# HGRN scores inside a hybrid encoder layer: levels 2 to 32 in blocks of 64 keys instead of 32

## The chip, the cores and the metric

The kernel runs on one core of a Trainium2 chip. A core has five engines that work beside each other and wait for each other by semaphores: PE (TensorE, matrix products; its weight loads are listed apart as PEld), DVE (VectorE), ACT (ScalarE), POOL (GpSimd) and SP (SyncE, which here issues DMAs). Products read SBUF and write PSUM, of which the kernel uses eight banks. The metric is the device time of one execution in microseconds (us), of which less is better.

## The reference, cut to what matters

One layer reads x (512 tokens, 2048 wide), projects it to all inputs of two mixers, RWKV-7 and HGRN2, joins their outputs and projects them back. HGRN2 has 8 heads of 128 key and 128 value dimensions. For each head the changed lines compute `att`, the scores of each token t against each earlier token s of the same stretch, with a decay per key dimension from s to t:

```python
b = jnp.cumsum(lf_c, axis=1)
diff = b[:, :, None] - b[:, None, :]
decay = jnp.where(causal, jnp.exp(jnp.where(causal, diff, 0.0)), 0.0)
att = jnp.einsum('btshd,bshd->btsh', q_c[:, :, None] * decay, k_c)
o_intra = jnp.einsum('btsh,bshv->bthv', att, i_c)
```

The decay differs by key dimension, so att is not one product of q and k. The kernel splits it by levels: at level w, a query in the second half of a stretch of 2w tokens meets a key in the first half, and the decay between them is the key's decay to the middle times the query's decay from the middle. With q and k scaled so, each level is a plain product. Level 1 joins neighbours, level 64 joins the two halves of 128 tokens; the diagonal (a token with itself) needs no decay.

## The kernel before

The projections are products of 128 by 128 weights with 512 columns, in fp32r, each made of three products of high and low parts (`three`, L431, and L1166 for the first ones). Between them lies the smaller work of the heads, in plain fp32. A program prints these functions below with their lines.

The order on every engine is fixed when the kernel is built, by a planner (class `Plan`). It keeps a clock for each engine, takes the next operation of each of several queues, and issues it when its inputs are ready by those clocks. An operation for PE goes between two projection products once its inputs are 0.35 us old; for products on part of the array (mode "narrow") it first waits a while so that several go together. `mm` gives a product's cost to the planner by its shape.

`hgrn_heads` works on two heads at once, so it runs four times (four pairs). For each head it holds q (`t` tile), f (the decays, later a copy of q or k), k, `near` (tag `nr`: the scores inside a small block, laid out as keys by queries), and later `dg` (a `t` tile with the scores of 4 stretches of 128 tokens).

- Level 1 and the diagonal: 16 products per head of 32 keys by 48 queries (32 undecayed and 16 decayed). Four lie side by side on the array, each writing 32 PSUM partitions (`blocks32`). The diagonal is cut out by a product with an identity of 32 columns, and level 1 is put in by `merge`.
- Then q and k are scaled from level to level (tensor_tensor, three per head and level). At every second level copies of q and k are kept (`kept`), so that two levels are multiplied in one PSUM bank (tag `mix`).
- Levels 2 and 4, then 8 and 16: per head and level 16 products of 32 keys by the 16 queries that lie in second halves, four side by side. Of the 32 x 16 scores only some belong to the level, and `merge` puts them in `near` by a copy under a mask (`cpred`, a table `hm` of one mask per level). After level 16 `near` is copied to the diagonal of `dg` in four parts of 32 partitions.
- Level 32: per head 8 products of 32 keys by 32 queries, which write partitions 0 to 31 and 64 to 95, so two lie side by side; two copies put them in `dg`. Level 64: per head 4 products of 64 by 64, two side by side, and two copies.
- `hgrn_out` multiplies `dg` with the values and adds the state of earlier stretches.

In the built program the projection products are `main` tiles, the heads' products `mix` (and `acc` in the RWKV scan). A whole-array product of the heads stands for RWKV state updates, transposes and the HGRN output.

Of the kernel before, what the change touches and what calls it, by code (L numbers as in the profile page):

```python
# [7 lines left out]
F32 = mybir.dt.float32  # L8
F32R = mybir.dt.float32r
U8 = mybir.dt.uint8  # L10
# [5 lines left out]
P = 128  # L16
T = 512
# [4 lines left out]
NHEAD = 8  # L22
C = 64
NCH = T // C
LEVELS = (1, 2, 4, 8, 16)
DECAY = math.exp(-0.5)
ALPHA = 2.0 ** 0.25
LN_EPS = 1e-5
# [206 lines left out]
def mixer_kernel(ctx, tc, head, x_r, w_all, par, up, ln_wb, consts, hmask, out):  # L235
# [72 lines left out]
    def mm(o, l, r, start=True, stop=True, **kw):  # L308
        m, n = size(l), size(r)
        narrow = m < P or l.shape[0] < P  # L310
        if r.dtype == F32R:
            cost = n / 2400 + 0.0135
        elif narrow:
            cost = 0.025 if m <= 32 else 0.06 if m <= 64 else 0.16
        else:
            cost = n / 600 + 0.005
        return Op([("pe", cost, lambda: pe.matmul(o, l, r, start=start, stop=stop, **kw))], [l, r], [o],  # L317
                  mode="narrow" if narrow else "main" if r.dtype == F32R else "whole")
# [20 lines left out]
    def tt(o, a, b, f=ALU.mult):  # L339
        return dve_op([a, b], o, lambda: dve.tensor_tensor(o, a, b, f),  # L340
                      base=0.16 if o.shape[0] < P and size(o) == C and o.tensor.name in tags else 0.07)
# [13 lines left out]
    def cpred(o, m, i):  # L355
        return dve_op([i], o, lambda: dve.copy_predicated(o, m, i))
# [142 lines left out]
        return u  # L499


    cst = cpool.tile([P, 3 * P + 32], F32, tag="cst", name="cst")
    ident = cst[:, 0:P]
    ones_blk = cst[:, P : 2 * P]
    mask_r = cst[:, 2 * P : 3 * P]
    eye32 = cst[:, 3 * P :]
    reset = cpool.tile([P, T], mybir.dt.bfloat16, tag="reset", name="reset")
    ones_r = cpool.tile([P, P], F32R, tag="ones_r", name="ones_r")
    hm = cpool.tile([P, 16 * len(LEVELS)], U8, tag="hm", name="hm")
    pr = cpool.tile([P, NPC], F32, tag="pr", name="pr")  # L510
    om = cpool.tile([P, 33], F32, tag="om", name="om")
    half = cpool.tile([P, 8, 8], F32, tag="half", name="half")
# [11 lines left out]
        return pr[:, base + p : base + p + 1]  # L524

    def constants():
        raw = st("ksq", [P, T])[:, : 16 * len(LEVELS)]
# [394 lines left out]
    def hgrn_heads(SS, h0):  # L922
# [4 lines left out]
        qqs, nrs = ([take(*a) for _ in SS] for a in (("q4", [P, 16, 48]), ("nr", [P, P])))  # L927
        totss = [[take("tot", [P, 256]) for _ in range(2)] for _ in SS]

        nears = [n.rearrange("p (c t) -> p c t", t=32) for n in nrs]  # L930
        for q, f, qq in zip(qs, fs, qqs):
            yield copy(qq[:, :, :32], q.rearrange("p (b t) -> p b t", t=32))
            yield tt(q, q, f)
            yield copy(qq[:, :, 32:], q.rearrange("p (b j two) -> p b j two", b=16, two=2)[:, :, :, 1])

        def blocks32(ps, n, k, moving):
            for b in range(16):
                c, g = b // 4, slice(b % 4 * 32, b % 4 * 32 + 32)
                yield mm(ps[g, c * n : c * n + n], k[:, b * 32 : b * 32 + 32], moving(b))

        def merge(near, m, w, scores):
            yield cpred(near.rearrange("p c (b two w) -> p c b two w", two=2, w=w)[:, :, :, 1],
                        hm[:, m * 16 : m * 16 + 16].rearrange("p (b w) -> p b w", w=w)[
                            :, None].to_broadcast([P, 4, 16 // w, w]),
                        scores.rearrange("p c (b w) -> p c b w", w=w))

        yield landed(*ks, *qqs)
        ps = take("mix")
        pss = [ps[:, 192 * i : 192 * i + 192] for i in range(2)]
        for pi, k, qq in zip(pss, ks, qqs):  # L950
            yield from blocks32(pi, 48, k, lambda b: qq[:, b])
        for pi, near in zip(pss, nears):
            scores = pi.rearrange("p (c t) -> p c t", t=48)
            yield tt(near, scores[:, :, :32], eye32[:, None, :].to_broadcast([P, 4, 32]))
            yield from merge(near, 0, 1, scores[:, :, 32:])
        drop(ps, *qqs)


# [1 line left out]
        for m, w in enumerate((2, 4, 8, 16, 32, 64, 128)):  # L960
# [13 lines left out]
            if w in (2, 8, 32):  # L974
# [2 lines left out]
                        halves = [a.rearrange("p (b two w) -> p b two w", two=2, w=w)[:, :, i] for a in (x, y)]  # L977
                        yield copy(*halves)
                continue
            if w == 16:  # L980
                yield room(t=2)
                dts = [take("t") for _ in SS]
                asking[0] -= 1
                dgs = [tiles(d) for d in dts]
                for d in dts:
                    yield memset(d, 0.0)
            yield landed(*qs, *ks, *kept)
            ps = take("mix")
            both = ((hw, kept, kept), (w, ks, qs))
            if w < 64:  # L990
                for v, (w1, k1, q1) in enumerate(both):
                    for i, (q, k) in enumerate(zip(q1, k1)):
                        yield from blocks32(ps[:, 64 * (2 * v + i) : 64 * (2 * v + i) + 64], 16, k,
                                            lambda b: q[:, b * 32 : b * 32 + 32].rearrange(
                                                "p (b two w) -> p b two w", two=2, w=w1)[:, :, 1])
                for v, (w1, k1, q1) in enumerate(both):
                    for i, near in enumerate(nears):
                        pi = ps[:, 64 * (2 * v + i) : 64 * (2 * v + i) + 64]
                        yield from merge(near, m + v, w1, pi.rearrange("p (c t) -> p c t", t=16))
# [4 lines left out]
            else:  # L1004

                for v, (w1, k1, q1) in enumerate(both):
                    n = P // (2 * w1)
                    for i, (q, k) in enumerate(zip(q1, k1)):
                        pi = ps[:, P * (2 * v + i) : P * (2 * v + i) + P]
                        for b in range(4 * n):  # L1010
                            c, o = b // n, b * 2 * w1
                            g = b % 2 * 64
                            at = (b // 2 if w1 == 64 else c) * w1
                            yield mm(pi[g : g + w1, at : at + w1], k[:, o : o + w1], q[:, o + w1 : o + 2 * w1])
                for v, (w1, k1, q1) in enumerate(both):
                    for i, dg in enumerate(dgs):
                        pi = ps[:, P * (2 * v + i) : P * (2 * v + i) + P]
                        for g in range(2):
                            part = pi[64 * g : 64 * g + w1].rearrange("p (c t) -> p c t", t=w1)
                            if w1 == 64:  # L1020
                                yield copy(dg[:64, g::2, 64:], part)
                            else:
                                yield copy(dg[64 * g : 64 * g + 32, :, 64 * g + 32 : 64 * g + 64], part)
            drop(ps)
            if w == 64:
                drop(*fs)
        drop(*nrs)
# [459 lines left out]
def _layout(inputs):  # L1487
# [48 lines left out]
    eye32 = e[:, None] % 32 == np.arange(32)  # L1536
    consts = np.concatenate([ident, blk, m, eye32], 1).astype(np.float32)
    hm = []
    for b in LEVELS:
        odd = np.arange(32).reshape(-1, 2, b)[:, 1].reshape(-1)  # L1540
        hm.append((e[:, None] % 32 // b == odd[None, :] // b - 1).astype(np.float32))
# [21 lines left out]
```

## Time and profile before

| | |
|---|---|
| median of 3 runs (lowest, highest) | 1066.27 us (1065.67, 1066.45) |
| the profiled execution's own time | 1066.34 us |
| its span, first to last instruction | 1064.5 us |
| mean granted TensorE clock | 0.997 |
| merges under a mask (COPY_PREDICATED) | 40, 8.3 us busy on DVE |
| products 128*32 with 16 queries, records | 1024 |
| products 128*32 with 32 queries, records | 128 |
| products 128*64 with 64 queries, records | 320 |

An fp32 product is two weight loads and two matmuls, so it makes two records on PE and two on PEld. Of a shape like 128*32 128x16, the first part is the tile of the array (rows times columns of the weights, here the keys) and the second what is streamed through it. Matmuls are pipelined: a record's duration overlaps the next ones, and starts tell more than durations.

### The profile page before, as it was taken

How to read it: one execution, taken by the hardware profiler on the slowest of the kernel's cores; microseconds unless marked ns; L12 is line 12 of the kernel's file. 1: busy time of each engine (PE TensorE's matmuls, PEld its weight loads, DVE VectorE, ACT ScalarE, POOL GpSimd, SP SyncE). 2: the span in 40 equal slices, each digit the busy share in tenths (PEclk: the TensorE clock that was granted, in tenths of full speed). 3: DMA queues.
4: the chain of work that ended last, by engine and by line, in shares of the span. 5: the costliest groups of instructions: out<-in, count | busy, mean ns of one | idle time of the engine just before them, and what ended most of it. 6: DMA issues, size and time to landing. Idle time of an engine off the chain costs nothing.

```text
span 1064.5 us, 18700 instructions
## 1 busy us (share of the span) xinstructions
PE 1050.1 (99%) x7418; PEld 873.6 (82%) x7418; DVE 742.3 (70%) x1616; ACT 460.0 (43%) x916; POOL 37.7 (4%) x81
## 2 busy tenths in 40 slices
PE   9999999999999999999999999999999999999995
PEld 8888888888888888888888888888888888888884
DVE  7466996577679678586996764557987876525556
ACT  6445334454453455355335543545345454323321
POOL 0000000000100000100000001000000011000000
PEclk9999999999999999999999999999999999999998
DMA  8122322232323222232231222323222244545613
GB/s 328 58 91 84 90 89 81 73 91 62 97 85 101 80 80 66 79 98 84 80 122 60 69 73 93 91 79 110 90 79 81 62 149 150 196 124 154 208 59 128
DMA packets 34934, 108.46 MB, mean 102 GB/s; under 512 B 4128, under 2 KB 5664, under 8 KB 34720
## 3 DMA queue, kind: packets, MB, share of 16 engines
q1 hardware_dynamic: 34704, 107.08, 31.8%
q8 instruction: 58, 0.95, 0.4%
q14 instruction: 28, 0.23, 0.1%
q10 hardware_dynamic: 144, 0.20, 0.1%
HBM read 99.92 MB, written 7.34 MB: 101 GB/s over the span
## 4 chain that ended last, share of the span: by engine, by line
PE 99%; DVE 1%; issue 0%; DVEq 0%
PE main L431 73%; PE mix L317 9%; PE mix L431 4%; PE acc L431 4%; PE main L1166 3%; PE mix L321 2%; PE main L317 2%; PE acc L317 1%; PE mix L1116 0%; DVE inv L349 0%; DVE inv L340 0%; DVE stats L1389 0%; DVEq L1559 0%; DVE mv L1331 0%; DVE mv L345 0%
## 5 line engine op out<-in xcount | busy, mean ns | idle before, releaser
L431 PE MATMUL main<-xh,wh 128*128 128x512 f32 x864 | 342.4, 396 | 0.0
L431 PE MATMUL main<-xh,wl 128*128 128x512 f32 x864 | 341.9, 396 | 0.0
L431 PE MATMUL main<-xl,wh 128*128 128x512 f32 x864 | 341.5, 395 | 0.0
L330 ACT ACTIVATE wh<-wr 128x512 fp32r<-128x512 f32 x299 | 186.0, 626 | 172.1 <-PE main L431 125.4
L340 DVE TENSOR_TENSOR wl<-wr,wh 128x512 fp32r<-128x512 f32 x299 | 203.8, 684 | 75.5 <-ACT wh L330 70.6
L431 PEld LDWEIGHTS main<-xh,wl 128*128 128x128 f32 x864 | 162.5, 188 | 32.2
L431 PEld LDWEIGHTS main<-xh,wh 128*128 128x128 f32 x864 | 162.4, 188 | 32.2
L431 PEld LDWEIGHTS main<-xl,wh 128*128 128x128 f32 x864 | 162.5, 188 | 31.8
L431 PE MATMUL main<-wl,xh 128*128 128x512 f32 x256 | 101.2, 395 | 0.0
L431 PE MATMUL main<-wh,xl 128*128 128x512 f32 x256 | 101.1, 395 | 0.0
L431 PE MATMUL main<-wh,xh 128*128 128x512 f32 x256 | 101.0, 395 | 0.0
L330 ACT ACTIVATE zz<-mix 64x64 f32<-64x64 f32 (+1 forms) x103 | 28.1, 273 | 69.5 <-PE mix L317 46.9
L431 PEld LDWEIGHTS main<-wh,xh 128*128 128x128 f32 x256 | 48.1, 188 | 10.2 <-DVE t L349 0.4
L431 PEld LDWEIGHTS main<-wh,xl 128*128 128x128 f32 x256 | 48.1, 188 | 9.5
L431 PEld LDWEIGHTS main<-wl,xh 128*128 128x128 f32 x256 | 48.1, 188 | 9.4
L340 DVE TENSOR_TENSOR inv<-inv 64x30 f32<-64x30 f32 (+14 forms) x120 | 38.6, 322 | 3.1
L340 DVE TENSOR_TENSOR inv<-inv,inv 64x30 f32<-64x30 f32 (+14 forms) x120 | 38.6, 322 | 2.9
L349 DVE SCALAR_TENSOR_TENSOR bd<-mix,pc,bd 64x64 f32<-64x64 f32 x112 | 31.0, 282 | 13.5 <-PE mix L317 12.2
L331 ACT ACTIVATE t<-main,om 128x512 f32<-128x512 f32 x33 | 22.4, 688 | 41.5 <-PE main L431 31.9
L349 DVE SCALAR_TENSOR_TENSOR t<-main,pr,t 128x511 f32<-128x511 f32 x33 | 24.3, 745 | 22.7 <-ACT t L331 22.6
L340 DVE TENSOR_TENSOR t<-t,tot 128x256 f32<-128x256 f32 x96 | 36.9, 417 | 0.2
L331 ACT ACTIVATE t<-main 128x512 f32<-128x512 f32 x32 | 18.7, 596 | 28.2 <-PE main L431 28.1
(239 smaller groups left out, 1364.7 us busy)
## 6 DMA issues: line engine op xcount, KB each, us to landing
wr<-w_all SPq DMA_DIRECT2D x156, 512.0 KB, 3.6
q<-head SPq DMA_DIRECT2D x15, 448.0 KB, 5.4
g<-x_r SPq DMA_DIRECT2D x16, 256.0 KB, 4.0
spill<-g SPq DMA_DIRECT2D x12, 256.0 KB, 3.9
t<-spill SPq DMA_DIRECT2D x12, 256.0 KB, 4.1
out<-q SPq DMA_DIRECT2D x12, 256.0 KB, 2.5
big<-ln_wb SPq DMA_DIRECT2D x1, 2048.0 KB, 8.7
up<-up SPq DMA_DIRECT2D x8, 128.0 KB, 2.8
```

The costliest lines, as they stand in the source:

```text
L317: return Op([("pe", cost, lambda: pe.matmul(o, l, r, start=start, stop=stop, **kw))], [l, r], [o], mode="narrow" if narrow else "main" if ...
L321: return Op([("pe", 0.11, lambda: pe.transpose(o, i, ident))], [i], [o])
L330: return "act", cost, lambda: sc_e.activation(o, i, f, scale=scale)
L331: return "act", cost, lambda: sc_e.activation(o, i, f, scale=scale, bias=bias)
L340: return dve_op([a, b], o, lambda: dve.tensor_tensor(o, a, b, f), base=0.16 if o.shape[0] < P and size(o) == C and o.tensor.name in tags e ...
L349: return dve_op([a, b], o, lambda: dve.scalar_tensor_tensor(o, a, s, b, f1, f2), per=0.00113, base=0.085 if o.shape[0] == P else 0.25 if s ...
L431: pe.matmul(ps, l, r, start=first and i == 0, stop=last and i == 2)
L1166: pe.matmul(pss[a], *ops, start=k == 0 and low == of == 0, stop=k == KT - 1 and low == 1)
```

## The change

Levels 2 to 32 now go in blocks of 64 keys: 8 products per head and level of 64 keys by the 32 queries in second halves, two side by side on the array. `near` is 64 wide (four stretches of 128 tokens, 64 queries each, on 128 partitions of keys). Level 1 keeps its 32-key products, but its scores are written twice, to both halves of the 64 queries, with an identity of 64 columns and a mask that keep the right one. Level 32 becomes one of the masked merges, so LEVELS and `hm` gain a level and `hm` is 32 columns a level. `dg` is taken at levels 32 and 64 instead of 8 and 16, gets the diagonal in two copies per head of 64 partitions, and level 64 as before. In the planner's cost table a product with up to 64 keys and at most 32 queries counts 0.03 instead of 0.06.

```diff
-LEVELS = (1, 2, 4, 8, 16)
+LEVELS = (1, 2, 4, 8, 16, 32)
...
-            cost = 0.025 if m <= 32 else 0.06 if m <= 64 else 0.16
+            cost = 0.025 if m <= 32 else 0.16 if m > 64 else 0.06 if n > 32 else 0.03
...
-        def blocks32(ps, n, k, moving):
-            for b in range(16):
-                c, g = b // 4, slice(b % 4 * 32, b % 4 * 32 + 32)
-                yield mm(ps[g, c * n : c * n + n], k[:, b * 32 : b * 32 + 32], moving(b))
+        def blocks(ps, m, k, moving):
+            n = size(moving(0))
+            for b in range(T // m):
+                c, g = b * m // P, slice(b * m % P, b * m % P + m)
+                yield mm(ps[g, c * n : c * n + n], k[:, b * m : b * m + m], moving(b))
...
-            scores = pi.rearrange("p (c t) -> p c t", t=48)
-            yield tt(near, scores[:, :, :32], eye32[:, None, :].to_broadcast([P, 4, 32]))
-            yield from merge(near, 0, 1, scores[:, :, 32:])
+            scores = pi.rearrange("p (c t) -> p c t", t=48)[:, :, None]
+            yield tt(near.rearrange("p c (h t) -> p c h t", h=2), scores[:, :, :, :32].to_broadcast([P, 4, 2, 32]),
+                     eye64.rearrange("p (h t) -> p h t", h=2)[:, None].to_broadcast([P, 4, 2, 32]))
+            yield cpred(near.rearrange("p c (h t two) -> p c h t two", h=2, two=2)[:, :, :, :, 1],
+                        mask(0, 16), scores[:, :, :, 32:].to_broadcast([P, 4, 2, 16]))
...
-            if w == 16:
+            if w == 64:
                 yield room(t=2)
                 dts = [take("t") for _ in SS]
...
-            both = ((hw, kept, kept), (w, ks, qs))
-            if w < 64:
-                for v, (w1, k1, q1) in enumerate(both):
-                    for i, (q, k) in enumerate(zip(q1, k1)):
-                        yield from blocks32(ps[:, 64 * (2 * v + i) : 64 * (2 * v + i) + 64], 16, k,
...
-                        if w1 == 16:
-                            for g in range(4):
-                                gs = slice(g * 32, g * 32 + 32)
-                                yield copy(dgs[i][gs, :, gs], near[gs])
...
+            parts = []
+            for m1, w1, k1, q1 in ((m, hw, kept, kept), (m + 1, w, ks, qs)):
+                for i, (q, k) in enumerate(zip(q1, k1)):
+                    pi = ps[:, P * len(parts) : P * len(parts) + P]
+                    parts.append((pi, i, m1, w1))
+                    if w1 < 64:
+                        yield from blocks(pi, C, k, lambda b: q[:, b * C : b * C + C].rearrange(
+                            "p (b two w) -> p b two w", two=2, w=w1)[:, :, 1])
+                        continue
+                    for b in range(4):
+                        o, g, at = b * P, b % 2 * 64, b // 2 * 64
+                        yield mm(pi[g : g + 64, at : at + 64], k[:, o : o + 64], q[:, o + 64 : o + P])
+            for pi, i, m1, w1 in parts:
+                if w1 < 64:
+                    yield cpred(later(nears[i], w1), mask(m1, w1),
+                                pi.rearrange("p (c b w) -> p c b w", c=4, w=w1))
+                    continue
+                for g in range(2):
+                    gs = slice(g * 64, g * 64 + 64)
+                    yield copy(dgs[i][gs, :, gs], nears[i][gs])
+                    yield copy(dgs[i][:64, g::2, 64:], pi[gs].rearrange("p (c t) -> p c t", t=64))
```

In the built program PE's rows for levels 2 and 4 of the first pair read as follows before (`main` are projection products, `mix` the PSUM bank of the levels, `t` the tiles of q and k; a size is that of the written part, x16 the number of equal rows):

```order
L431 MATMUL main_1293<-wh_1509,xh_77 128x512
L431 MATMUL main_1293<-wl_1510,xh_77 128x512
L317 MATMUL mix_1540<-t_1093 32x16 x16
L317 MATMUL mix_1540<-t_1295 32x16 x16
L317 MATMUL mix_1540<-t_972,t_1094 32x16 x16
L317 MATMUL mix_1540<-t_1204,t_1296 32x16 x16
L431 MATMUL main_1293<-wh_1509,xl_93 128x512
```

And at the same place of PE's queue in the changed kernel:

```order
L431 MATMUL main_1302<-wh_1508,xh_77 128x512
L431 MATMUL main_1302<-wl_1509,xh_77 128x512
L317 MATMUL mix_1543<-t_1093 64x32 x8
L317 MATMUL mix_1543<-t_1295 64x32 x8
L317 MATMUL mix_1543<-t_972,t_1094 64x32 x8
L317 MATMUL mix_1543<-t_1204,t_1296 64x32 x8
L431 MATMUL main_1302<-wh_1508,xl_93 128x512
```

The block moves by three projection products and stays in one piece; its 64 products of 32 by 16 are 32 of 64 by 32. Levels 8 and 16 change in the same way.

PE's rows for levels 32 and 64 of the same pair, before:

```order
L431 MATMUL main_1302<-wh_1772,xl_98 128x512
L317 MATMUL mix_1812<-t_1093 32x32 x8
L317 MATMUL mix_1812<-t_1295 32x32 x8
L317 MATMUL mix_1812<-t_972,t_1094 64x64 x4
L317 MATMUL mix_1812<-t_1204,t_1296 64x64 x4
L431 MATMUL main_1317<-wh_1772,xh_82 128x512
```

And now:

```order
L431 MATMUL main_1325<-wh_1637,xh_81 128x512
L317 MATMUL mix_1726<-t_1093 64x32 x8
L317 MATMUL mix_1726<-t_1295 64x32 x8
L317 MATMUL mix_1726<-t_972,t_1094 64x64 x4
L317 MATMUL mix_1726<-t_1204,t_1296 64x64 x4
L431 MATMUL main_1325<-wl_1638,xh_81 128x512
```

Level 32 keeps its 16 products, now with 64 keys each; level 64 is the same, and the block stands some projection products earlier.

DVE's rows for the merges of levels 8 and 16 of that pair, before (`nr` is `near`, `hm` the masks):

```order
L340 TENSOR_TENSOR wl_1657<-wr_1514,wh_1656 128x512
L356 COPY_PREDICATED nr_1307<-hm,mix_1665 128x8x8
L356 COPY_PREDICATED nr_1308<-hm,mix_1665 128x8x8
L356 COPY_PREDICATED nr_1307<-hm,mix_1665 128x4x16
L382 COPY t_1652<-nr_1307 32x4x32 x2
L340 TENSOR_TENSOR wl_1743<-wr_1514,wh_1742 128x512
L356 COPY_PREDICATED nr_1308<-hm,mix_1665 128x4x16
L340 TENSOR_TENSOR t_972<-t_972,tot_1310 128x16x16
```

And now:

```order
L340 TENSOR_TENSOR wl_1638<-wr_1516,wh_1637 128x512
L356 COPY_PREDICATED nr_1307<-hm,mix_1634 128x16x8
L356 COPY_PREDICATED nr_1308<-hm,mix_1634 128x16x8
L356 COPY_PREDICATED nr_1307<-hm,mix_1634 128x8x16
L356 COPY_PREDICATED nr_1308<-hm,mix_1634 128x8x16
L340 TENSOR_TENSOR t_972<-t_972,tot_1310 128x16x16
```

Each merge has twice the elements, and the small copies to `dg` have left this place.

More of the change, by code (lines that the diff above doesn't have):

```diff
@@ L499, in unit @@
         return u
-    cst = cpool.tile([P, 3 * P + 32], F32, tag="cst", name="cst")
+    cst = cpool.tile([P, 3 * P + C], F32, tag="cst", name="cst")
     ident = cst[:, 0:P]
@@ L505, in mixer_kernel @@
     mask_r = cst[:, 2 * P : 3 * P]
-    eye32 = cst[:, 3 * P :]
+    eye64 = cst[:, 3 * P :]
     reset = cpool.tile([P, T], mybir.dt.bfloat16, tag="reset", name="reset")
     ones_r = cpool.tile([P, P], F32R, tag="ones_r", name="ones_r")
-    hm = cpool.tile([P, 16 * len(LEVELS)], U8, tag="hm", name="hm")
+    hm = cpool.tile([P, 32 * len(LEVELS)], U8, tag="hm", name="hm")
     pr = cpool.tile([P, NPC], F32, tag="pr", name="pr")
@@ L526, in constants @@
     def constants():
-        raw = st("ksq", [P, T])[:, : 16 * len(LEVELS)]
+        raw = st("ksq", [P, T])[:, : 32 * len(LEVELS)]
         for t, a in ((pr, par), (cst, consts), (raw, hmask)):
@@ L926, in hgrn_heads @@
         qs, fs, ks = ([S[n] for S in SS] for n in "qfk")
-        qqs, nrs = ([take(*a) for _ in SS] for a in (("q4", [P, 16, 48]), ("nr", [P, P])))
+        qqs = [take("q4", [P, 16, 48]) for _ in SS]
+        nears = [take("nr", [P, 4, C]) for _ in SS]
         totss = [[take("tot", [P, 256]) for _ in range(2)] for _ in SS]
-        nears = [n.rearrange("p (c t) -> p c t", t=32) for n in nrs]
         for q, f, qq in zip(qs, fs, qqs):
@@ L934, in hgrn_heads, with later, mask @@
             yield copy(qq[:, :, 32:], q.rearrange("p (b j two) -> p b j two", b=16, two=2)[:, :, :, 1])
-        def blocks32(ps, n, k, moving):
-            for b in range(16):
-                c, g = b // 4, slice(b % 4 * 32, b % 4 * 32 + 32)
-                yield mm(ps[g, c * n : c * n + n], k[:, b * 32 : b * 32 + 32], moving(b))
[L941 to L945, printed above, removed]
+        def blocks(ps, m, k, moving):
[3 more added lines that the diff above has]
+                yield mm(ps[g, c * n : c * n + n], k[:, b * m : b * m + m], moving(b))
+        def later(x, w):
+            return x.rearrange("p c (b two w) -> p c b two w", two=2, w=w)[:, :, :, 1]
+        def mask(m, w):
+            return hm[:, m * 32 : m * 32 + 32].rearrange("p (b w) -> p b w", w=w)[:, None].to_broadcast(
+                [P, 4, 32 // w, w])
         yield landed(*ks, *qqs)
@@ L950, in hgrn_heads @@
         for pi, k, qq in zip(pss, ks, qqs):
-            yield from blocks32(pi, 48, k, lambda b: qq[:, b])
+            yield from blocks(pi, 32, k, lambda b: qq[:, b])
         for pi, near in zip(pss, nears):
-            scores = pi.rearrange("p (c t) -> p c t", t=48)
-            yield tt(near, scores[:, :, :32], eye32[:, None, :].to_broadcast([P, 4, 32]))
-            yield from merge(near, 0, 1, scores[:, :, 32:])
+            scores = pi.rearrange("p (c t) -> p c t", t=48)[:, :, None]
[3 more added lines that the diff above has]
+                        mask(0, 16), scores[:, :, :, 32:].to_broadcast([P, 4, 2, 16]))
         drop(ps, *qqs)
@@ L988, in hgrn_heads @@
             ps = take("mix")
-            both = ((hw, kept, kept), (w, ks, qs))
-            if w < 64:
-                for v, (w1, k1, q1) in enumerate(both):
-                    for i, (q, k) in enumerate(zip(q1, k1)):
-                        yield from blocks32(ps[:, 64 * (2 * v + i) : 64 * (2 * v + i) + 64], 16, k,
[L994 to L999, printed above, removed]
-                        if w1 == 16:
-                            for g in range(4):
-                                gs = slice(g * 32, g * 32 + 32)
-                                yield copy(dgs[i][gs, :, gs], near[gs])
[L1004 to L1023, printed above, removed]
@@ L1026, in hgrn_heads @@
                 drop(*fs)
-        drop(*nrs)
+        drop(*nears)
         for i, S in enumerate(SS):
@@ L1535, in _layout @@
     m = np.where(e[None, :] < 64, np.where(e[:, None] < 64, -strict, strict), (s <= t))
-    eye32 = e[:, None] % 32 == np.arange(32)
-    consts = np.concatenate([ident, blk, m, eye32], 1).astype(np.float32)
+    eye64 = e[:, None] % 64 == np.arange(64)
+    consts = np.concatenate([ident, blk, m, eye64], 1).astype(np.float32)
     hm = []
     for b in LEVELS:
-        odd = np.arange(32).reshape(-1, 2, b)[:, 1].reshape(-1)
-        hm.append((e[:, None] % 32 // b == odd[None, :] // b - 1).astype(np.float32))
+        odd = np.arange(64).reshape(-1, 2, b)[:, 1].reshape(-1)
+        hm.append((e[:, None] % 64 // b == odd[None, :] // b - 1).astype(np.float32))
     hm = np.concatenate(hm, 1)
```

## The prediction

> **What bounds the kernel now.** I read the page first: the engines' busy shares, then the chain that ended last, then what TensorE (PE) waited for.
>
> ```profile
> span 1064.5 us, 18700 instructions
> PE 1050.1 (99%) x7418; PEld 873.6 (82%) x7418; DVE 742.3 (70%) x1616; ACT 460.0 (43%) x916; POOL 37.7 (4%) x81
> PE 99%; DVE 1%; issue 0%; DVEq 0%
> PE mix L317 <- issue: 2.4, 3, 1.1
> PE mix L1116 <- DVE inv L1114: 1.1, 1, 1.1
> ```
>
> The second line is busy time, the third the chain by engine, the last two all that PE waited for (us in total, times, longest). PE sets the end alone: it waits 1.1 us for another engine in the whole span, at the start. So the time changes by what the change adds to or takes from PE's own queue, and by nothing on VectorE (DVE), ScalarE (ACT) or the DMAs while they stay as early as they are. The odd row is the 2.4 us "issue", in three pieces, in products of the changed lines; it comes back below.
>
> A matmul's own duration is no price here, since they overlap. The price is the time from the start of one block of products to the start of what follows on PE. These are the timeline rows of the first pair of heads (start, length, engine, line, out<-in, shape; one fp32 product makes two records):
>
> ```profile
> 162.17 0.72 PE L317 MATMUL mix<-t 128*32 128x16 f32 x63
> ...
> 163.43 0.50 PE L431 MATMUL main<-wh,xl 128*128 128x512 f32 x1
> ...
> 169.55 0.71 PE L317 MATMUL mix<-t 128*32 128x16 f32 x62
> ...
> 170.75 0.50 PE L431 MATMUL main<-wl,xh 128*128 128x512 f32 x1
> ...
> 179.61 0.70 PE L317 MATMUL mix<-t 128*32 128x32 f32 x32
> 180.24 0.69 PE L317 MATMUL mix<-t,t 128*64 128x64 f32 x16
> 180.85 0.50 PE L431 MATMUL main<-wh,xh 128*128 128x512 f32 x1
> ...
> 259.70 2.08 PE L317 MATMUL mix<-zz,big 128*64 128x64 f32 x64
> 261.72 0.50 PE L431 MATMUL main<-xh,wl 128*128 128x512 f32 x1
> ```
>
> Levels 2 and 4 (64 products of 32 keys by 16 queries, four side by side) take 163.43 - 162.17 = 1.26 us. Levels 8 and 16, the same shapes, take 1.20. Level 32 (16 products of 32 by 32, of which only two lie side by side) takes 0.63, and level 64 (8 products of 64 by 64, two side by side) 0.61. The last block is another part of the kernel, the RWKV outputs: 32 products with 64 stationary columns, two side by side, in 2.02.
>
> **The price of the new products.** They have 64 keys and 32 queries, two side by side. No row has that shape, so I price it from its neighbours. The 64 by 64 blocks give (2.02 - 0.61) / (32 - 8) = 0.0588 us a product, and 0.61 - 8 x 0.0588 = 0.14 for the end of a block (the last product's tail and the change back to whole-array work). With that 0.14, the old blocks cost (1.20 - 0.14) / 64 = 0.0166 a product with four side by side, and (0.63 - 0.14) / 16 = 0.031 with two. What counts is how long one strip of the array is held by one product: 4 x 16.6 = 66 ns for 32 keys by 16 queries, 2 x 31 = 61 ns for 32 by 32, 2 x 58.8 = 118 ns for 64 by 64. Twice the queries cost nothing at 32 keys, so streaming the queries is not the limit there. Twice keys and queries cost twice. The weight loads (PEld) say which of the two it is:
>
> ```profile
> L317 PEld LDWEIGHTS mix<-t 128*32 128x32 f32 x640 | 7.5, 110 | 3.2 <-issue 2.0 <-DVE wl L340 0.4 <-PE main L431 0.4
> L317 PEld LDWEIGHTS mix<-zz,big 128*64 128x64 f32 x256 | 7.8, 138 | 1.3 <-issue 0.7 <-PE main L431 0.4 <-ACT t L331 0.2
> L317 PEld LDWEIGHTS mix<-zz,q 128*128 128x128 f32 x112 | 19.1, 190 | 2.9
> ```
>
> A load of 32 columns lasts 110 ns, of 64 138, of 128 190: 28 ns for 32 more columns, 52 for 64 more, about 0.85 ns a column above a fixed latency. A product loads its keys twice (two records), so a strip is loading for 2 x 32 x 0.85 = 54 ns with 32 keys and 2 x 64 x 0.85 = 109 with 64. The measured 61 to 66 and 118 lie 7 to 12 ns above that, at 16 queries as at 32. So I take it that a strip is held by the loading of its keys, that fewer queries than keys save nothing, and that a product of 64 keys by 32 queries costs what 64 by 64 costs: **0.0588 us**. The bounds from both sides are 0.031 (the 32 by 32 row) and 0.0588 (the 64 by 64 row).
>
> The Trainium skill's page "TensorE: Matmul & The Clock Gate", section "LDWEIGHTS (loading the stationary operand)", states that a load takes its columns divided by 1.2 in ns, whatever the rows: 53.3 ns for 64 columns. That speaks against this change and agrees with the 28 and 52 ns above. An estimate by that figure alone, two loads to a strip and two strips, is 0.0533 us a product, which in the sum below makes 1069.3 us.
>
> **The sum on PE.** The order of after.py keeps twelve such blocks of levels above 1, three to each of four pairs, each in one piece. Level 1 keeps its shape. Per pair:
> - Levels 2 and 4: 32 products, 32 x 0.0588 + 0.14 = 2.02 in place of 1.26, so +0.76.
> - Levels 8 and 16: 2.02 in place of 1.20, so +0.82.
> - Levels 32 and 64: 24 products of 64 keys, 24 x 0.0588 + 0.14 = 1.55 in place of 180.85 - 179.61 = 1.24, so +0.31. The change of tile shape between the two levels goes with it.
>
> That is +1.89 a pair, **+7.56 us** for four. With a price p in us for the new product the whole term is 320 p - 11.24, which I use for the rivals.
>
> Three of the eight old blocks of 64 products carry a stall:
>
> ```profile
> 399.35 0.71 PE L317 MATMUL mix<-t 128*32 128x16 f32 x62
> ...
> 401.63 0.25 PE L317 MATMUL mix<-t,t 128*32 128x16 f32 x5 [1.05 <-issue]
> 401.81 0.49 PE L317 MATMUL acc<-bd,q 128*128 128x128 f32 x2
> ...
> 590.03 0.72 PE L317 MATMUL mix<-t 128*32 128x16 f32 x63
> ...
> 591.98 0.25 PE L317 MATMUL mix<-t,t 128*32 128x16 f32 x6 [0.73 <-issue]
> 592.16 0.51 PE L431 MATMUL main<-wh,xl 128*128 128x512 f32 x1
> ...
> 846.92 0.71 PE L317 MATMUL mix<-t 128*32 128x16 f32 x62
> ...
> 848.63 0.32 PE L317 MATMUL mix<-t,t 128*32 128x16 f32 x15 [0.57 <-issue]
> 848.87 0.50 PE L431 MATMUL main<-xl,wh 128*128 128x512 f32 x1
> ```
>
> These blocks last 2.46, 2.13 and 1.95 us instead of 1.26, 1.26 and 1.20: 1.20 + 0.87 + 0.75 = 2.82 us too long. Nothing in the program is waited for there. The DMA view of 589.3 to 592 has next to nothing but an instruction fetch:
>
> ```profile
> q8 instruction: 1, 0.02, 2.0%
> ```
>
> So I read the stalls as PE running out of fetched instructions while it eats 64 products in about a microsecond. The new blocks have half the instructions and, at my price, use them more slowly. The outputs block at 259.70 has the same 32 products at that pace and no gap. I count all three stalls as gone: **-2.82 us**; the bounds are 0 and -2.82.
>
> Sum: +7.56 - 2.82 = +4.74. It is made against the profiled execution's own time, 1066.34 us, which is 0.07 from the median of the runs (1066.27). The forecast is 1071.1 us.
>
> **What I cost at nothing.** The merges:
>
> ```profile
> L356 DVE COPY_PREDICATED nr<-hm,mix 128x64 f32<-128x64 uint8 x40 | 8.3, 255 | 12.2 <-PE mix L317 11.8
> L340 DVE TENSOR_TENSOR nr<-mix,cst 128x128 f32<-128x128 f32 x8 | 2.3, 288 | 3.0 <-PE mix L317 3.0
> L340 DVE TENSOR_TENSOR t<-t,tot 128x256 f32<-128x256 f32 x96 | 36.9, 417 | 0.2
> L330 ACT ACTIVATE t<-nr 32x128 f32<-32x128 f32 x19 | 5.9, 308 | 14.4 <-DVE nr L356 8.7 <-DVE sm L345 4.5 <-DVE sm L346 1.0
> L382 DVE COPY t<-nr 32x128 f32<-32x128 f32 x13 | 2.9, 220 | 0.5
> ```
>
> 40 merges of 64 elements become 48 of 128; at the 288 ns of the 128-element row that is 13.8 us in place of 8.3. The eight first products with the identity go from 288 to about 417 (+1.0). The 32 small copies of the diagonal blocks (8.8 us on two engines) and the 16 of level 32 become 16 of 256 elements. DVE gains a few us over the span. Its cover is the 30% of the span in which it is idle, and PE never waits for it at those places. If that cover is gone, each of the twelve merges delays PE by no more than the extra of its four copies, 4 x 0.03 to 4 x 0.08 us: 1.4 to 3.8 in all; below nothing it cannot go, since there is no such wait to save. Two `t` tiles per pair are claimed later (level 64 instead of 16) with their memsets on POOL, whose busy share is 4%; that frees buffers and could only hold back an evacuation that the planner orders otherwise, which I price at 0. The constants grow by 144 columns and load while PE runs 33 us of products without a break (a row of the chain in order of time):
>
> ```profile
> 5.26 32.95 PE main L1166 x144
> ```
>
> **Rivals.**
> 1. *Faster: a strip has a floor per product that does not depend on its keys.* The 61 and 66 ns fit a floor as well as a load. Then 64 keys by 32 queries cost 2 x 31 to 2 x 33 ns a strip, p = 0.032, the term is 320 x 0.032 - 11.24 = -1.0, and with the stalls gone the time is 1066.34 - 1.0 - 2.82 = 1062.5. The price decides: the whole change is nil at p = 14.06 / 320 = 0.0439. Against it: the load rows grow with the columns, and twice the loading is 92% of the strip's time at 64 keys as well. For it: no row has more keys than queries at 64 keys. The skill's page "TensorEngine Tiling (Array Packing)", section "Instruction Overhead", states such a floor of about 60 cycles for any free size up to 60; the 61 and 66 ns cannot refute it.
> 2. *No difference:* loads overlap in part and p lies between 0.037 and 0.051, about 1066.
> 3. *The stalls come back elsewhere,* since fetches fall at other places of the queue: 1066.34 + 7.56 = 1073.9. Against it: no block of the slower kind shows one now.
> 4. *PE now waits for the merges:* 1071.1 + 1.4 to 3.8, about 1073.5. The 1.1 us of waits in the whole span speak against it.
>
> **How the numbers follow.** Forecast 0.70, rival 1 0.18, rival 2 0.05, rival 3 0.05, rival 4 0.02. A measurement tells about 0.2% (2.1 us) from no change. So slower is 0.70 + 0.05 + 0.02, less 0.02 for a forecast that comes out small: 0.75; faster 0.18; same 0.05 + 0.02 = 0.07. The range has to reach rival 1, whose chance is near two in ten alone: from 1061.5 to 1073.0. The forecast's own range is 1069.3 to 1072.5.
>
> **What would show it.** In the trace of after, blocks of 32 products 128*64 by 128x32 that last about 2.0 us, those of levels 32 and 64 about 1.55, and no "issue" wait in them. Blocks of 1.1 to 1.2 us would make the price wrong and rival 1 right; "issue" gaps elsewhere in the line rival 3; waits of PE for DVE or ACT in the chain rival 4.

## The result, and the profile after

| | before | after |
|---|---|---|
| median of the runs beside each other | 1065.97 us (1065.59 to 1066.45, 4 runs) | 1071.16 us (1070.86 to 1071.68, 4 runs) |
| the profiled execution's own time | 1066.34 us | 1070.89 us |
| its span | 1064.5 us | 1069.1 us |
| mean granted TensorE clock | 0.997 | 0.997 |

The ratio of after to before is 1.0051, with a 95% interval of 1.0039 to 1.0064: the change makes the kernel slower by half a per cent.

The page of after: span and instructions, busy time of the engines, and the chain that ended last by engine.

```profile
span 1069.1 us, 17668 instructions
...
PE 1057.2 (99%) x6906; PEld 880.6 (82%) x6906; DVE 748.4 (70%) x1622; ACT 454.3 (42%) x886; POOL 38.8 (4%) x81
...
PE 99%; DVE 1%; DVEq 0%; issue 0%
```

PE has 512 records fewer and is busy 7.1 us longer, with the same share of the span. All that PE waited for in after (total, times, longest in us) is one row, the known wait at the start:

```profile
PE mix L1110 <- DVE inv L1108: 1.1, 1, 1.1
```

The 2.4 us of "issue" are gone. The timeline of after, PE alone (start, length, engine, line, out<-in, tile, streamed shape, records), at the levels of the first pair and at two places where before had a stall:

```profile
162.98 1.12 PE L317 MATMUL mix<-t 128*64 128x32 f32 x32
163.94 1.10 PE L317 MATMUL mix<-t,t 128*64 128x32 f32 x32
164.97 0.50 PE L431 MATMUL main<-wh,xl 128*128 128x512 f32 x1
...
179.42 1.13 PE L317 MATMUL mix<-t 128*64 128x32 f32 x32
180.38 0.66 PE L317 MATMUL mix<-t,t 128*64 128x64 f32 x16
180.97 0.50 PE L431 MATMUL main<-wl,xh 128*128 128x512 f32 x1
...
402.39 1.12 PE L317 MATMUL mix<-t 128*64 128x32 f32 x32
403.35 1.10 PE L317 MATMUL mix<-t,t 128*64 128x32 f32 x32
404.38 0.49 PE L317 MATMUL mix<-rt,big 128*128 128x128 f32 x2
...
850.37 1.12 PE L317 MATMUL mix<-t 128*64 128x32 f32 x32
851.33 1.10 PE L317 MATMUL mix<-t,t 128*64 128x32 f32 x32
852.36 0.49 PE L317 MATMUL mix<-rt,big 128*128 128x128 f32 x2
```

A block of 32 new products lasts 164.97 - 162.98 = 1.99 us, in the first pair as at 402 and 850 us; levels 32 and 64 together last 180.97 - 179.42 = 1.55. From the first start to the last, the starts of the 32 products lie 59.0 ns apart.

The groups of after that answer to the merges and their neighbours of before (busy us, mean ns, idle time before them):

```profile
L356 DVE COPY_PREDICATED nr<-hm,mix 128x128 f32<-128x128 uint8 x48 | 14.1, 348 | 21.7 <-PE mix L317 21.3
...
L340 DVE TENSOR_TENSOR nr<-mix,cst 128x256 f32<-128x256 f32 x8 | 3.4, 422 | 3.0 <-PE mix L317 3.0
```

They cost DVE 6.9 us more, and DVE as a whole 6.1, without one new wait on PE.

**Where the time went.** I added up PE's starts, block by block, in both traces. The eight blocks of levels 2 to 16 take 12.58 us before and 15.91 after (+3.33); the four of levels 32 and 64 take 0.305 us more each (+1.22). That is +4.55, and the two profiled executions differ by 1070.89 - 1066.34 = 4.55. The products with 512 columns, nearly all of them projections, total 923.09 us before and 923.12 after.

### The profile page after: what moved, and what is told of

It is laid out like the page before. It is cut to its first block, busy times and chain, and to the rows that moved or that the text cites. A ratio compares the mean times of both kernels' runs of the same rounds, so it can differ in the third digit from the quotient of the medians.

```text
span 1069.1 us, 17668 instructions
## 1 busy us (share of the span) xinstructions
PE 1057.2 (99%) x6906; PEld 880.6 (82%) x6906; DVE 748.4 (70%) x1622; ACT 454.3 (42%) x886; POOL 38.8 (4%) x81
## 4 chain that ended last, share of the span: by engine, by line
PE 99%; DVE 1%; DVEq 0%; issue 0%
PE main L431 72%; PE mix L317 10%; PE mix L431 4%; PE acc L431 4%; PE main L1160 3%; PE mix L321 2%; PE main L317 2%; PE acc L317 1%; PE mix L1110 0%; DVE inv L349 0%; DVE inv L340 0%; DVE stats L1383 0%; DVEq L1553 0%; DVE mv L1325 0%; DVE mv L345 0%
## 5 line engine op out<-in xcount | busy, mean ns | idle before, releaser
L330 ACT ACTIVATE zz<-mix 64x64 f32<-64x64 f32 (+1 forms) x91 | 25.9, 285 | 62.1 <-PE mix L317 39.7
L372 POOL TENSOR_TENSOR sm<-sm,mhalf 128x8 f32<-128x8 f32 x8 | 13.8, 1731 | 469.3 <-DVE sm L346 469.3
```

The source lines that it names most:

```text
L330: return "act", cost, lambda: sc_e.activation(o, i, f, scale=scale)
L372: lambda: pool.tensor_tensor(o, i, mhalf[:, : size(o)], ALU.pow))], [i], [o])
```

## The experiments

Each kernel differs from before or after by one thing. A median stands with the ratio to before, measured beside it, and its 95% interval; where block times are given, they are worked out from starts in one profiled execution.

### 1 and 2: half and twice the queries to a product

The first kernel is after with 16 queries a product, and its merges shrink with them; the second takes all 64 queries of a block. Of the added lines the one marked 16 stands in the first kernel and the one marked 64 in the second.

```diff
-                        yield from blocks(pi, C, k, lambda b: q[:, b * C : b * C + C].rearrange(
-                            "p (b two w) -> p b two w", two=2, w=w1)[:, :, 1])
+                        yield from blocks(pi, C, k, lambda b: q[:, b * C + 32 : b * C + 48])     # 16
+                        yield from blocks(pi, C, k, lambda b: q[:, b * C : b * C + C], ps, P * (len(parts) - 1))     # 64
...
```

> The changed kernel, but a product of levels 2 to 32 takes 16 queries instead of 32 (64 keys as before; it leaves out half the queries of these levels). Theory (a strip of the array is held while its 64 keys are loaded): nothing changes, 0.0588 us a product, the block of levels 2 and 4 stays at 2.0 us and the time at 1071 us, within 0.5. Rival A (streaming the queries holds the strip): half the streaming, the block falls to about 1.1 us and the time by 320 x 0.027 = 8.6 us to 1062.5.

> The changed kernel, but a product of levels 2 to 32 takes all 64 queries of its stretch instead of 32 (64 keys as before; the results run over each other, so the scores of these levels are left out). Theory (loading 64 keys holds the strip, and 64 queries stream in no longer than that, as in the 64 by 64 products): 1071 us, within 0.5, block still 2.0 us. Rival A (streaming holds the strip at 32 queries already): twice the streaming, +0.0588 us a product, 1071 + 18.8 = 1090 us. Rival B (a fixed time for each product on a 64-column tile): 1071 us, as the theory.

Measured: 1072.05 us, 1.0058 (1.0043 to 1.0073), with 16 queries; 1070.95 us, 1.0047 (1.0031 to 1.0064), with 64. PE's timeline with 16 queries:

```profile
163.59 1.11 PE L317 MATMUL mix<-t 128*64 128x16 f32 x32
164.54 1.09 PE L317 MATMUL mix<-t,t 128*64 128x16 f32 x32
165.57 0.50 PE L431 MATMUL main<-wh,xl 128*128 128x512 f32 x1
```

And with 64:

```profile
163.46 1.15 PE L317 MATMUL mix<-t 128*64 128x64 f32 x32
164.44 1.10 PE L317 MATMUL mix<-t,t 128*64 128x64 f32 x32
165.47 0.50 PE L431 MATMUL main<-wh,xl 128*128 128x512 f32 x1
```

The block lasts 1.98 us with 16 queries, 1.99 with 32, 2.01 with 64. The starts lie 59.0, 59.0 and 59.9 ns apart. From 16 to 64 queries the streaming makes 0.9 ns of difference. The first kernel's time is 0.9 us above after's, more than the half microsecond expected; its profiled execution has one wait of PE for ACT, 0.9 us at 877 us, that after does not have.

### 3 and 5: 48 keys instead of 64

Both load only 48 of a block's 64 keys in levels 2 to 32. In the third kernel a merge needs two copies for that, one for each half of the partitions; the fifth merges only the first half, so it has as many merges as after.

```diff
-                yield mm(ps[g, c * n : c * n + n], k[:, b * m : b * m + m], moving(b))
+                kk = k[:, b * m : b * m + (48 if m == C else m)]
+                yield mm(ps[slice(g.start, g.start + size(kk)), c * n : c * n + n], kk, moving(b))
...
+                    for g in range(2):     # the fifth kernel: range(1)
+                        gs = slice(g * 64, g * 64 + 48)
```

> The changed kernel, but a product of levels 2 to 32 loads only 48 of its 64 keys, on the same 64-column tile, with the same 32 queries and the same count of products (it leaves out a quarter of the keys of these levels). Theory (loading holds the strip, about 0.85 ns a key, twice a product): 2 x 48 x 0.85 + 9 = 91 ns a strip, 0.0455 us a product, 320 x 0.0133 = 4.3 us less: 1066.9 us, block of levels 2 and 4 at 32 x 0.0455 + 0.14 = 1.6 us. Rival A (streaming) and rival B (a fixed time for each product on a 64-column tile): no change, 1071 us, 2.0 us.

> As the run with 48 of 64 keys a product, but with the count of merges of the changed kernel: only the keys of the first 64 partitions are merged (it leaves out a quarter of the keys in the products of levels 2 to 32 and the other half of the keys in their merges). Theory (the run before it was slow because its 40 merges more on DVE came late for PE, not because of its products, whose blocks fell to 1.56 us): no wait of PE for DVE of 0.5 us or more in the middle of the span, blocks 1.56 us, 1071 - 4.3 = 1066.9 us. Rival (something else in these products delays PE): 1070 us or more.

Measured: 1074.87 us, 1.0084 (1.0069 to 1.0099), for the third; 1066.78 us, 1.0012 (1.0003 to 1.0021), for the fifth. PE's timeline of the fifth:

```profile
163.17 0.91 PE L317 MATMUL mix<-t 128*48 128x32 f32 x32
163.91 0.89 PE L317 MATMUL mix<-t,t 128*48 128x32 f32 x32
164.73 0.50 PE L431 MATMUL main<-wh,xl 128*128 128x512 f32 x1
```

The block takes 1.56 us and the starts lie 45.7 ns apart, in both kernels. 16 keys fewer save 59.0 - 45.7 = 13.3 ns, 0.83 ns a key: a strip is held 1.66 ns for each key it loads, at two loads a product. So the price goes with the keys, and twelve cheaper blocks bring the fifth kernel to 4.4 us below after (4.1 when each is taken against the before measured beside it); 4.3 had been expected.

The third has the same products and yet is 8.1 us slower than the fifth, where 1066.9 had been expected of it. Its DVE makes 40 merges more. What PE waited for in the third:

```profile
PE main L431 <- DVE wl L340: 1.9, 2, 1.6
...
PE mix L317 <- DVE rt L349: 0.7, 2, 0.5
PE acc L317 <- DVE bd L349: 0.5, 2, 0.3
```

Its busy times by stretches (stretch, PE busy with records, granted clock, DMA share, GB/s), around the longest of these waits:

```profile
870.00:874.50 4.50, 4.41 (x21) 1.00 0.66 241
874.50:876.70 2.20, 0.57 (x2) 1.00 0.00 0
876.70:880.00 3.30, 3.29 (x8) 0.50 0.65 192
880.00:884.00 4.00, 4.00 (x19) 0.98 0.51 170
```

PE stands idle for some 1.6 us, and then runs 3.3 us at half clock. The chain that led to this wait goes through merges, then a reload of `t` from `spill` that took 3.86 us and merges again. The waits shown (3.1 us) and the half clock (some 1.6 us) make up 4.7 of the 8.1 us; where the rest lies was not worked out. The miss was mine: I had not priced the doubled merges. It bounds the cover that the prediction relied on: DVE, idle 30% of the span, takes 6 us more without a wait (after) and not 24 (the third, 766.1 us busy).

### 4: the new scheme with products of 32 keys

After, with levels 2 to 32 as twice as many products of 32 keys by the same 32 queries, four side by side.

```diff
-                        yield from blocks(pi, C, k, lambda b: q[:, b * C : b * C + C].rearrange(
+                        yield from blocks(pi, 32, k, lambda b: q[:, b // 2 * C : b // 2 * C + C].rearrange(
```

> The changed kernel with each product of levels 2 to 32 cut in two along its keys: 640 products of 32 keys by 32 queries, four side by side, for the same scores; everything behind them is as in the changed kernel. Theory (loading holds the strip): a strip takes 61 to 66 ns, 0.0160 us a product, 0.032 for what cost 0.0588: 8.6 us less, 1062.5 us without stalls. By the places of the instruction fetches (one for every 256 of PE's instructions, and a stall where a block of 256 begins just behind such a place) one of its eight blocks of 64 products should stall, by about 1.2 us, the first block of the fourth pair: 1063.7 us. Rival A (streaming holds the strip): two streams of 32 queries in four strips cost what one cost in two, 1071 us. Rival C (the stalls have nothing to do with fetches): 1062.5, or stalls in other blocks.

Measured: 1067.42 us, 1.0018 (1.0009 to 1.0028); slower than before by two parts in a thousand, and 3.7 us under after. Of its eight blocks of levels 2 to 16 the first two last 1.28 us and five 1.23. The remaining one, at 835 us, has a stall, and a second one stands behind another block; both in PE's timeline:

```profile
419.19 0.40 PE L431 MATMUL main<-xh,wh 128*128 128x512 f32 x1
420.91 0.39 PE L431 MATMUL main<-xl,wh 128*128 128x512 f32 x1 [1.33 <-issue]
...
834.93 0.73 PE L317 MATMUL mix<-t 128*32 128x32 f32 x62
...
837.51 0.22 PE L317 MATMUL mix<-t,t 128*32 128x32 f32 x1 [1.30 <-issue]
837.66 0.50 PE L431 MATMUL main<-xh,wh 128*128 128x512 f32 x1
```

The stall at 837 us was forecast, the one at 421 was not; each makes the next start 1.5 us late. Without them the 1067.4 would be near 1064.4, where the forecast without stalls was 1062.5: the twelve blocks save some 7.0 us against after and not 8.6. So products of 32 keys bring the blocks nearly back to their old length with the new merges, for which PE waits nowhere, but with 64 products to a block the stalls come back.

### 6 and 7: the kernel before, its instructions shifted

PE's queue fetches its instructions in pieces. In before the fetch queue has 58 fetches of 16 KB for the 14,973 PE instructions in the trace, 256 to a piece, and each of the three stalls lies at instruction 193 of a piece, counted from PE's first instruction. So I shifted all later instructions, by one warm-up product less and 26 (8) small ones more: 100 (28) instructions.

```diff
-    WARM, T0 = 9, 4.2
+    WARM, T0 = 8, 4.2
...
+    for n in range(26):     # the seventh kernel: range(8)
+        g = slice(n % 4 * 32, n % 4 * 32 + 32)
+        pe.matmul(warm[g, 0:1], zero[:, 0:32], zero[:, 0:1])
```

> The kernel before, with 100 instructions more on PE at its start: one warm-up product less and 26 small ones of 32 keys by 1 more. Every later instruction has the same order and moves by 100 places against the fetches of 256. Theory (the three stalls are fetches that come due just behind the start of a block of 256 instructions): no block of 64 products begins just behind a fetch any more, all eight last 1.2 to 1.3 us and the time falls by 2.8 us to 1062.6 to 1063.2. Rival (the stalls belong to these products or to their data): the same three blocks stall, 1065.4 to 1066 us.

> The kernel before, with 28 instructions more on PE at its start (one warm-up product less, 8 small ones more). Theory of the fetches: the stalls move. The first blocks of the second and third pairs lose theirs; the second block of the first pair (at about 169.5 us, 1.20 us long before) gets one of about 1.2 us; the second block of the fourth pair (at about 847) keeps a small one of 0.3 to 0.5. In all 1.6 instead of 2.8 us: about 1 us less than before, 1064.4 to 1065. Rival (the stalls belong to these products): the same three blocks as before, no change.

Measured: 1066.23 us, 1.0003 (0.9994 to 1.0012), for 100; 1066.21 us, 1.0008 (0.9999 to 1.0017), for 28. Neither median fell; 1062.6 to 1063.2 and 1064.4 to 1065 had been expected. The profiled execution with 100 took 1063.96 us. Its blocks at the former places:

```profile
589.01 0.72 PE L317 MATMUL mix<-t 128*32 128x16 f32 x63
...
590.21 0.50 PE L431 MATMUL main<-wh,xl 128*128 128x512 f32 x1
...
846.06 0.18 PE L317 MATMUL mix<-t 128*32 128x16 f32 x1 [0.38 <-issue]
```

The block at 589 us takes 1.20 us now, that at 400 too, and one stall is left, at 846 us and again at instruction 193. With 28, the stalls lie in the blocks at 170, 400, 591 and 847 us, by 0.38, 1.07, 0.27 and 0.59 us, all four at 193 again. Two of the four, at 400 and 591 us, had been expected to go. A position in the queue thus says where a stall may fall, but not whether it does. Why the median with 100 stood still stayed open here and is taken up by runs 9 to 11.

### 8 and 12: level 32 four side by side, in the kernel before

The only level blocks of before that left half the array unused are those of level 32. Here its two heads take turns and fill all four strips; the eighth kernel has the shift by 100 as well, the twelfth has not.

```diff
+                    if w1 == 32:
+                        turn = [(i, 2 * j + e) for j in range(2 * n) for i in range(2) for e in range(2)]
...
-                            g = b % 2 * 64
+                            g = b % 2 * 64 + (32 * i if w1 == 32 else 0)
```

> The kernel before with the 100 instructions more at PE's start, and with level 32 four side by side: the 32 by 32 products of the second head write partitions 32 to 63 and 96 to 127 and stand in turn with those of the first, in place of two side by side. Theory (a strip is held for 61 to 66 ns by 32 keys, whatever lies beside it): level 32 falls from 0.63 to about 0.38 us a pair, 1.0 us in all, on top of the run without stalls: 1061.8 us. Rival (products side by side delay each other when they stream 32 queries each): no change against the run with 100 more, 1062.9 us.

> The kernel before, without any shift of the first products, with level 32 alone changed: its 16 products of 32 keys by 32 queries lie four side by side, the two heads in turn, where they lay two side by side. Nothing else differs and no instruction is added. If a strip is held for the loads of 32 keys and the four strips run beside each other, the four level 32 blocks go from 0.63 to 0.38 to 0.40 us, 0.92 to 1.0 us in all, and the median is 1064.8 to 1065.2 against 1065.97; the stalls near 400, 591 and 848 us stay as they vary (0 to 1.3 us each), since PE's instruction count ahead of them is the same. If the strips share a limit, the blocks stay at 0.63 and the time is that of before.

Measured: 1064.78 us, 0.9994 (0.9985 to 1.0002), with the shift; 1065.02 us, 0.999 (0.9981 to 0.9999), without. The eighth was expected at 1061.8; its profiled execution (1065.28) has a stall of 1.16 us at 847 us and the slow start described below. PE's timeline of the twelfth:

```profile
433.38 0.46 PE L317 MATMUL mix<-t 128*32 128x32 f32 x32
433.77 0.69 PE L317 MATMUL mix<-t,t 128*64 128x64 f32 x16
```

Level 32 takes 433.77 - 433.38 = 0.39 us where it took 0.63; four times that is 0.96 us, and the medians differ by 1065.99 - 1065.02 = 0.97. This version beats both kernels, by as little as the interval says: it runs from 0.1 to 2.0 us, so that the two figures agree this well is in part luck. The shorter blocks themselves stand in the trace.

### 9 to 11: the shift on after, and second executions of before

The ninth is after with the shift by 100, the tenth is before and the eleventh before with the shift, both unchanged.

> The kernel after, with its first products shifted by 100 PE instructions (one warm-up product of 512 columns less, 26 small ones more), the same shift as in the run of before with 100. Control for the stalls: if PE only runs out of instructions where 256 of them are used up in less than some 2.5 us, the blocks of 128 instructions in 1.98 us lie on the safe side wherever the fetches fall: no issue wait above 0.2 us in any level block, all eight of them 1.97 to 2.03 us from start to next start, and the time is that of after, 1070.6 to 1071.8, with its narrow spread. If it was luck of position that after shows no stall, some block is 0.3 us or more longer and the time is 1071.5 to 1073.

> The kernel before, unchanged, for a second profiled execution. Its recorded execution has three stalls, 2.82 us in all. If a stall is a property of the position in PE's queue alone, the same three blocks (near 400, 591 and 848 us) are long again by 0.87 to 1.20 us together 2.8 us and the time is 1066.0 to 1066.7. If the fetch competes with the DMA traffic of the moment, the places stay (instruction 193 mod 256) but the sizes change by half a microsecond or more, and the time goes with their sum: 1063.5 plus the sum.

> The kernel before shifted by 100 PE instructions, unchanged, for a second profiled execution. The first look had one stall of 0.56 us and took 1063.96 us, while the median of its 11 runs is 1066.23. If the missing 2 us of the slower executions are stalls, a slower execution shows long level blocks or issue gaps that sum to its time less 1063.4; if they are something else (projection products slower, waits for DVE or ACT, a later start) the level blocks stay at 1.20 us and the time lies elsewhere in the trace.

Measured: 1071.04 us, 1.0051 (1.0037 to 1.0065); 1065.62 us, 0.9997 (0.9987 to 1.0007); 1065.66 us, 0.9998 (0.9988 to 1.0008).

In the tenth, the three blocks that had stalls, in PE's timeline:

```profile
402.09 0.25 PE L317 MATMUL mix<-t,t 128*32 128x16 f32 x5 [1.14 <-issue]
...
590.47 0.70 PE L317 MATMUL mix<-t 128*32 128x16 f32 x62
...
591.67 0.50 PE L431 MATMUL main<-wh,xl 128*128 128x512 f32 x1
...
848.39 0.32 PE L317 MATMUL mix<-t,t 128*32 128x16 f32 x15 [0.81 <-issue]
```

The same program stalls at two of the three places, by 1.34 and 0.99 us over an undisturbed 1.20: 2.33 us in all, where the first execution lost 2.93. The twelfth, whose queue has as many instructions ahead of them, has 0.97, 0.11 and 1.26: 2.34.

The traces also show when each fetch landed, and with it how long a stall is. In before the fetches ahead of the three stalls landed at 400.24, 590.28 and 847.17 us, and the stalls end at 401.63, 591.98 and 848.63. All 14 stalls of over half a microsecond in the traces end 1.3 to 1.7 us after the landing of the fetch ahead of them. At 591 us in the tenth run instruction 193 starts 1.49 us after that landing, in time, and there is no stall. With the first fetch set against the second piece, the second against the third and so on, no instruction 193 in the 14 traces starts less than 1.25 us after its fetch landed. A stall is thus as long as PE is ahead of its fetch.

In the eleventh, the first projection products (they read `xh` and `xl`):

```profile
5.61 2.93 PE L1169 MATMUL main<-xh,t 128*128 128x512 f32 x6
8.33 1.48 PE L1169 MATMUL main<-xl,t 128*128 128x512 f32 x3
```

In the sixth, the same program, they are twice as fast:

```profile
5.49 1.65 PE L1169 MATMUL main<-xh,t 128*128 128x512 f32 x6
6.99 0.85 PE L1169 MATMUL main<-xl,t 128*128 128x512 f32 x3
```

By 10 us the eleventh is 2.1 us late, and of its 2.76 us more than the sixth (1066.72 against 1063.96) only 0.25 is a longer stall. The slow start goes with the clock. The trace's first record of the granted clock, of 1.00, begins at 10.1 us in the eleventh and at 5.3 us in the sixth; the mean over the span counts the time before it as 1.00, though nothing is recorded there. Up to that record the projection products start 0.43 us apart, as at the recorded 0.50 of the third run, and from it on 0.23. It is so in all 14 traces: where products go at half pace at the start, they do so until the first record of the clock. That record begins at 4.2 to 7.2 us in the ten traces of kernels without the 26 small products, and at 5.3, 9.1, 10.1 and 10.4 us in the four with them (runs 6, 8, 11 and 9). Its other runs fall into two groups, 1064.30 to 1064.65 (4 runs) and 1066.66 to 1066.89 (3 runs), some 2.3 us apart. So the shift does take most of the stalls away, but the small products that make it go with a full clock that comes late in some executions. That the group near 1066.8 is slow for the same reason is argued from the distance; only one of its runs has a trace.

The ninth shows the same slow start (its profiled execution took 1073.38 us; the other four runs 1070.96 to 1071.36), and its level blocks are those of after:

```profile
165.52 1.12 PE L317 MATMUL mix<-t 128*64 128x32 f32 x32
166.47 1.10 PE L317 MATMUL mix<-t,t 128*64 128x32 f32 x32
167.51 0.50 PE L431 MATMUL main<-wh,xl 128*128 128x512 f32 x1
```

All eight last 1.99 us and no "issue" wait is left, with the fetches at other places. So after has no stall at either of two positions of its queue.

## Why the prediction was right

- **The bound.** PE alone sets the end in both kernels: the whole 4.55 us lie in the level blocks.
- **The price, 0.0588 us a product.** Measured 0.0590. The reason given, that a strip is held by loading its keys, was put to the test from three sides: a quarter to all of the queries made no difference of more than 0.9 ns, 48 keys cost 45.7 ns, and 32 keys four side by side cost 17.2 ns, a strip of 69 ns. The strip's 69, 91 and 118 ns for 32, 48 and 64 keys follow the keys. That it is the loading and no other work that grows with the keys is argued, from the load rows, which grow by 28 ns for 32 columns and 52 for 64.
- **The Trainium skill's figure** for the loads ("TensorE: Matmul & The Clock Gate", "LDWEIGHTS (loading the stationary operand)"), 1/1.2 = 0.83 ns a column, is the 0.83 ns a key between after and run 5, and the 1069.3 made from it alone was low by the 5 to 6 ns a product that lie between 53.3 and 59.0.
- **The blocks.** 2.02 was forecast and 1.99 measured, since the end of a block is worth 0.10 and not 0.14; 1.55 was met. An undisturbed block of before takes 1.20 at levels 2 and 4 too, except in the first pair (1.25), where the prediction put 1.26 for all four. The products term is so 15.91 - 9.65 + 4 x 0.305 = +7.48, for +7.56.
- **The stalls.** -2.82 was forecast as gone, and gone they are; by the corrected 1.20 they held 12.58 - 9.65 = 2.93 us of the profiled execution. 7.48 - 2.93 = 4.55. What the prediction left out is that this term differs from execution to execution: with the 2.33 us of the tenth run it would be +5.15, and the medians differ by 5.19. The 1071.1 can be this near because after has no such term, but that it is within 0.1 us of the median is in part luck: against after's profiled execution (1070.89) it is 0.2 too high, and the median lies 0.27 above this execution, which no term of the sum foresaw. The size of the change was forecast 0.45 us too small.
- **The cause of the stalls,** PE running out of fetched instructions, is shown as to place: every stall of over half a microsecond that the profile calls "issue" lies at instruction 193 (once 194) of 256, in before and in runs 4, 6 to 8 and 10 to 12, and there is none where a block of 128 instructions takes 1.99 us. It is shown as to length too, by the landings of the fetches (under runs 9 to 11). What decides when a fetch begins, and so why the length differs from execution to execution, is open.
- **The merges at nothing.** DVE was given "a few us" and got 6.1; PE did not wait. The third run shows the end of that cover.
- **The rivals.** A floor independent of the keys, 1062.5, is refuted by the 59.0 ns of after and by runs 3 and 5: equal queries, fewer keys, shorter blocks. Loads overlapping in part is refuted by 0.0590. Stalls elsewhere did not come, and the ninth run shows the same with the fetches at other places. Waits for merges did not come either, though the third run makes them with twice the merges.

## What to carry to other kernels

For small fp32 products with several strips side by side, price the loads: columns of weights a strip loads, twice a product, and do not count on shorter streaming to pay for them. Here filling idle strips (level 32 four side by side) gained 0.97 us, where larger products with half as many side by side lost 5. A stall that one profile shows is a sample: look at a second execution before its length goes into a sum, look when the fetch ahead of it landed, and shift instructions before you believe in its place.

## What the runs showed of the hardware

- In these traces the pieces of 256 PE instructions held PE up only in or just behind blocks that use them fast: a level block of before uses 256 instructions in 1.20 us. A fetch's landing and instruction 193 of the piece lie at least 1.25 us apart. The same program stalled at three of the places in one execution and at two in another, by other lengths.
- A standstill of PE can cost more than its length: in the third run, after 1.6 us without work, the granted clock was 0.50 for 3.3 us, and a projection product took 0.43 us instead of 0.23. The two idle pieces of 1.3 us in run 4 left the clock at 1.00.
- A mean granted clock can hide a slow start. Before the first record of the clock some projection products ran at half pace in 12 of the 14 traces, and the mean over the span counts that time as full clock. In three of the four traces with 26 small products at the start the full clock came at 9.1 to 10.4 us, in all others by 7.2; the eleventh run was 2.1 us late by 10 us. Why it came early in the fourth stays open.
